# A decoder block on one core: tokens in the order of their expert groups, two tiles finished among the last pairs, rows moved by index

## The chip, the cores and the metric

One core of a Trainium2 chip runs the whole kernel in one launch. The metric is the device time of that launch in microseconds (us), the median of several runs. The engines are TensorE (PE in the profile), VectorE (DVE), ScalarE (ACT), GpSimd (POOL) and SyncE (SP), which here only starts transfers.

## The reference, cut to what matters

512 tokens of width 1024. Two token mixers come first (a chunked retention and a sliding-window attention); the change leaves them alone. Then a mixture of experts in two levels, and last a gated embedding per layer:

```python
g_sel = argmax(softmax(hf @ w_rg + b_rg))             # one of 4 groups
top_p, top_i = top_k(softmax(e_logits[g_sel]), 2)     # 2 of the 8 experts of that group
for grp in range(4):                                  # 8 experts each, D=1024, F=256
    hid = silu(hf @ w_gate) * (hf @ w_up)
    y += (hid * combine) @ w_down
x = x + y
ple = rms_norm(p @ w_ple, g)                          # p: 512 x 256
x = x + sigmoid(rms_norm(x, g2) @ w_ple_gate) * ple   # the gate product, 1024 x 1024
```

## The kernel before

**Stages.** The mixers and their output projection run until about 378 us; the result x1 (four tiles of 128 tokens) stays in SBUF and a copy of it goes to DRAM (`X1`). Then 16 pairs of experts (p_ = 0 to 15; pair p_ holds experts p_ and p_ + 16), then a tail with the gate product of the four tiles.

**A pair.** A pair has 64 slots for each of its two experts. Its 128 rows of x1 are gathered from `X1` by index on POOL (`fetch`, L1062), two pairs ahead. TensorE transposes them (`turn`, L1073), VectorE applies the gain (`turned`, `grow`, L962). `gu` (L1182) computes gate and up in plain fp32, the two experts in the two halves of the array's columns; `hidden` applies SiLU on ScalarE (L1195) and the product on VectorE (L1196); `ht` (L1203) transposes, VectorE copies (L1205); `down` (L1226) computes the output. For pairs 0 to 11 (`SC = 12`) ScalarE and VectorE copy the output (L1241, L1239) and POOL scatters its rows by index to `Y` in DRAM (L1246). For pairs 12 to 15 the output is split into a high and a low part in fp32r, and `combine` (L1256) brings its rows to the four token tiles by products with one-hot matrices, which `added` adds to x2 (L1269). In this kernel x2 is x1, tile by tile.

**Y.** In pair 12 `collect` clears eight tiles on VectorE (L1498) and gathers the rows of `Y` into them (L1503), two per token tile. POOL adds the two (`presum`, L1510), VectorE adds the sum to x2 (`total`, L1515).

**Embedding.** p arrives transposed (`pT`); `ple_split` splits it, and `embed(t)` computes p @ w_ple and its norm for one tile in each of the pairs 10 to 13 (twelve products of 512 columns in the split form, L1304 to L1306).

**Tail.** For each tile `tail_a` transposes x2 (L1430) and splits it (L1434, L1436), `tail_r` computes the norm, `tail_b` the gate product (L1456) in two halves of 512 columns as three fp32r products (high by high, low by high, high by low; 24 instructions for a half), `tail_c` applies the sigmoid (L1464) and writes the rows from SP (L1467). The gate weights (`wpg`, four loads of 1 MB) are split by `wpsplit` into two tiles of their own: ScalarE copies the high part (L1408), POOL (for the fourth VectorE) subtracts (L1410).

**What sets the order.** Each engine works in the order in which the program is written; waits are by semaphore. The weights come by SP in the order of `want`, each into a free place of SBUF as soon as the program frees one (`pump`, L322 and L324); `KEEP` sets places aside from a pair on, and `AT` and `at=` name places. A place that was another tile's makes the new writer wait for that tile's last user. `overflow` (L1321), after pair 0's gate product, is a branch for experts with more than 64 tokens, which is not taken here; SP reads a count for it, and its tiles have places of their own.

## Time and profile before

| | us |
|---|---|
| median of 3 runs | 692.26 (691.82 to 693.97) |
| the profiled execution | 694.86 |
| its span, first to last instruction | 693.1 |
| TensorE busy (share of the span) | 650.2 (94%) |
| VectorE, ScalarE, POOL busy | 319.5, 201.4, 91.9 |
| gate product of pair 0 starts | 378.78 |
| down of pair 15 starts | 628.90 |
| mean granted TensorE clock | 0.986 |

The timelines give for each piece of work its start, its length (matmuls overlap, so a group's length is up to 0.4 longer than the time to its successor), and how long the engine was idle before it and for whom. The waits add this up.

### The profile page before, as it was taken

To read this page: it belongs to the slowest core of one execution; us is meant where nothing else is said; L and a number is where in the kernel's file an instruction comes from. 1 tells how busy PE (TensorE), PEld (TensorE's weight loads), DVE (VectorE), ACT (ScalarE), POOL (GpSimd) and SP (SyncE) were. 2 spreads that over 40 slices of the span, in tenths; PEclk is the share of its full clock that TensorE was granted. 3 is DMA by queue.
4 is the path that set the end of the run, shared out by engine and by line. 5 is a ranking of instruction groups with operands and counts; after the bars stand their busy time and mean duration, and the time that the engine had idled before them with its cause. 6 is when DMAs were issued, how large, how long until landed. Compare 5 with 4: busy or idle time off the path is not lost. (4 is left out here: it accounts for less than half of the span.)

```text
span 693.1 us, 8410 instructions
## 1 busy us (share of the span) xinstructions
PE 650.2 (94%) x3210; PEld 441.8 (64%) x3210; DVE 319.5 (46%) x697; ACT 201.4 (29%) x393; POOL 91.9 (13%) x75
## 2 busy tenths in 40 slices
PE   7999999999999999999999699899879997998997
PEld 6768888778888888888887243333324443433886
DVE  5395556652456425635148121321202236566762
ACT  6664352363133334330142000000002110106431
POOL 1005000000001000000000121111105115417200
PEclk9999999999999999999999899999999999999999
DMA  8726310531204731049878489999999999992011
GB/s 282 283 85 238 143 61 1 182 122 62 114 22 169 304 122 61 0 183 354 347 293 341 152 305 415 420 418 421 418 421 421 414 374 413 417 415 90 31 47 45
DMA packets 32476, 162.98 MB, mean 235 GB/s; under 512 B 5577, under 2 KB 8265, under 8 KB 16304
## 3 DMA queue, kind: packets, MB, share of 16 engines
q1 hardware_dynamic: 26672, 149.90, 54.8%
q0 software_dynamic: 5040, 10.39, 4.0%
q10 hardware_dynamic: 720, 2.11, 0.8%
q8 instruction: 26, 0.43, 0.2%
q14 instruction: 18, 0.15, 0.1%
HBM read 155.67 MB, written 14.68 MB: 246 GB/s over the span
## 5 line engine op out<-in xcount | busy, mean ns | idle before, releaser
L431 PE MATMUL bank<-slab,slab 128*128 128x512 f32 x320 | 126.4, 395 | 0.0
L433 PE MATMUL bank<-slab,slab 128*128 128x512 f32 x320 | 124.9, 391 | 0.5 <-DVE slab L348 0.5
L1182 PE MATMUL bank<-slab,slab 128*64 128x512 f32 x512 | 119.9, 602 | 5.7 <-DMA slab<-wgu 4.2
L432 PE MATMUL bank<-slab,slab 128*128 128x512 f32 x320 | 125.0, 391 | 0.0
L1182 PEld LDWEIGHTS bank<-slab,slab 128*64 128x64 f32 x512 | 39.0, 138 | 80.1 <-issue 69.2
L348 DVE TENSOR_TENSOR slab<-slab,slab 128x1024 fp32r<-128x1024 f32 (+2 forms) x50 | 53.9, 1092 | 57.5 <-ACT slab L347 42.6
L431 PEld LDWEIGHTS bank<-slab,slab 128*128 128x128 f32 x320 | 60.1, 188 | 14.1 <-issue 1.8
L433 PEld LDWEIGHTS bank<-slab,slab 128*128 128x128 f32 x320 | 60.1, 188 | 13.6 <-DVE slab L348 1.0
L432 PEld LDWEIGHTS bank<-slab,slab 128*128 128x128 f32 x320 | 60.2, 188 | 11.6
L1226 PE MATMUL bank<-slab,slab 128*64 128x512 f32 x256 | 60.9, 618 | 5.1 <-DVE slab L1205 5.1
L347 ACT ACTIVATE slab<-slab 128x1024 fp32r<-128x1024 f32 (+2 forms) x50 | 46.4, 952 | 56.7 <-PE bank L432 26.1
L1196 DVE SCALAR_TENSOR_TENSOR slab<-slab,st,bank 128x256 f32<-128x256 f32 x16 | 7.7, 480 | 104.4 <-ACT slab L1195 104.4
L1195 ACT ACTIVATE slab<-bank,st 128x256 f32<-128x256 f32 x16 | 7.6, 474 | 146.2 <-PE bank L1182 138.5
L1456 PE MATMUL bank<-slab,slab 128*128 128x512 f32 (+1 forms) x216 | 45.9, 369 | 1.4 <-DVE slab L1436 1.4
L1456 PEld LDWEIGHTS bank<-slab,slab 128*128 128x128 f32 x216 | 37.0, 189 | 9.0 <-DVE slab L1436 2.3
L1226 PEld LDWEIGHTS bank<-slab,slab 128*64 128x64 f32 x256 | 18.3, 141 | 37.0 <-issue 36.3
L1062 POOL DMA_INDIRECT slab<-X,st x15 | 15.4, 1030 | 108.9 <-PE bank L1073 81.1
L880 PE MATMUL bank<-slab,slab 128*128 128x512 f32 x64 | 26.1, 408 | 0.0
L355 POOL TENSOR_TENSOR st<-st,ct 128x4 f32<-128x4 f32 x4 | 4.4, 1104 | 159.6 <-DVE st L354 159.6
L882 PE MATMUL bank<-slab,slab 128*128 128x512 f32 x64 | 25.0, 391 | 0.0
L881 PE MATMUL bank<-slab,slab 128*128 128x512 f32 x64 | 24.9, 390 | 0.0
L1239 DVE COPY slab<-bank 128x512 f32<-128x512 f32 x12 | 8.3, 692 | 34.6 <-PE bank L1226 34.6
(248 smaller groups left out, 924.5 us busy)
## 6 DMA issues: line engine op xcount, KB each, us to landing
slab<-wgu SPq DMA_DIRECT2D x64, 1024.0 KB, 13.9
slab<-wd SPq DMA_DIRECT2D x31, 1024.0 KB, 12.7
slab<-win SPq DMA_DIRECT2D x17, 1024.0 KB, 4.9
slab<-x SPq DMA_DIRECT2D x8, 512.0 KB, 6.1
Y<-slab SPq DMA_DIRECT2D x8, 512.0 KB, 4.9
slab<-wout SPq DMA_DIRECT2D x4, 1024.0 KB, 5.6
slab<-wpg SPq DMA_DIRECT2D x4, 1024.0 KB, 14.6
slab<-wso SPq DMA_DIRECT2D x2, 1024.0 KB, 6.1
```

Source lines behind the costliest of these rows:

```text
L347: A.activation(H.r(*shape), rawap, AF.Copy)
L348: (eng or V).tensor_tensor(L.r(*shape), rawap, H.f(*shape), op=OP.subtract)
L431: T.matmul(ps, wh[:, k, :], hh[k], start=(k == 0), stop=False)
L432: T.matmul(ps, wh[:, k, :], hl[k], start=False, stop=False)
L433: T.matmul(ps, wl[:, k, :], hh[k], start=False, stop=(k == nk - 1))
L880: T.matmul(ps, a, wh[:, kk, :], start=(k == 0), stop=False)
L881: T.matmul(ps, a, wl[:, kk, :], start=False, stop=False)
L882: T.matmul(ps, b, wh[:, kk, :], start=False, stop=(k == 7))
L1062: G.indirect_dma_start(out=XR[p_].f(1024), out_offset=None, in_=X1, in_offset=bass.IndirectOffsetOnAxis(ap=toki[:, p_:p_ + 1], axis=0), bo ...
L1182: T.matmul(b[j * 64:(j + 1) * 64, :], xg[:, k, j * 64:(j + 1) * 64], load(("gu", p_ + 16 * j, k // 4)).f(4, 512)[:, k % 4, :], start=(k == ...
L1226: T.matmul(bs[nh][j * 64:(j + 1) * 64, :], t.f(2, P)[:, f, j * 64:(j + 1) * 64], load(("wd", p_ + 16 * j)).f(2, 1024)[:, f, nh * 512:(nh + ...
L1456: T.matmul(b, (H, L, H)[i][:, k, :], w, start=(k, i) == terms[0], stop=(k, i) == terms[-1])
```

## The change

- **Pairs.** Pair p_ holds experts 2 p_ and 2 p_ + 1, so pairs 0 to 3 are group 0, and so on; the router's columns are no longer reordered. Tokens get a new order, by group: `order_a`, `order_b` and `order_c` (after pairs 2 and 3, and in pair 4) compute each token's place, the row index of each new tile (`permi`), the index of its `Y` rows (`yi`) and the place of every slot for the one-hot matrices.
- **Rows by index.** x1's tiles in SBUF are freed before pair 0. p is gathered by index (`ple_rows`) and transposed on TensorE (`ple_split`); embeddings move to pairs 7 to 9. x2 is gathered per new tile (`rows_x`), `Y` rows per tile (`rows_y`, two gathers): tile 0 in pair 9, tiles 1 and 2 in pair 12, tile 3 after pair 13; `total` adds both on POOL (tile 3: VectorE). The output rows are scattered by POOL.
- **Gate product of tile 0** after down in pairs 11 and 12 in plain fp32 from the raw weights (`tail_x`, `tail_b`, `tail_c`); tile 1's first half in pair 15.
- **Combine** only for tiles 2 and 3.
- **Weights.** `wpg` comes after pair 8 into places 42 to 57; `wpsplit` writes the low part over the raw weights and runs after pair 14 (0 and 1) and inside pair 15's gate product (2 and 3). `KEEP` begins earlier. `overflow`'s tiles have other places.

```diff
...
     SC = 12
-    KEEP = {9: (46, 74)}
-    AT = {("gu", 0, 1): 0, ("gu", 16, 1): 4, ("gu", 1, 0): 14, ("gu", 17, 1): 18}
-    LATE = (("gu", 16, 1),)
-    PL, PU = 8, (10, 11, 12, 13)
+    KEEP = {4: (58, 74), 6: (42, 82)}
+    AT = {("gu", 0, 1): 0, ("gu", 1, 1): 4, ("gu", 2, 0): 14, ("gu", 3, 1): 18}
+    LATE = (("gu", 1, 1),) + tuple(("wpg", i) for i in range(4)) + (("gple",), ("wple",))
+    PL, PU, PG = 5, {7: (0,), 8: (1, 2), 9: (3,)}, 8
...
     for p_ in range(16):
         for j in range(2):
-            for e in (p_, p_ + 16):
+            for e in (2 * p_, 2 * p_ + 1):
                 want(("gu", e, j), I["wgu"][e, j], 8, AT.get(("gu", e, j)))
-        for i in range(WE if p_ == 15 else 0):
-            want(("wpg", i), I["wpg"][i], 8)
-        for e in (p_, p_ + 16):
+        for e in (2 * p_, 2 * p_ + 1):
             want(("wd", e), I["wd"][e], 8)
         if p_ == PL:
-            want(("pT",), I["pT"], 4)
-            want(("gple",), 1024, 4)
-            want(("wple",), I["wple"], 8)
-    for i in range(WE, 4):
-        want(("wpg", i), I["wpg"][i], 8)
+            want(("gple",), 1024, 4, 60)
+            want(("wple",), I["wple"], 8, 62)
+        if p_ == PG:
+            for i in range(4):
+                want(("wpg", i), I["wpg"][i], 8, 42 + 4 * i)
...
+        for i in range(2):
+            V.tensor_reduce(few[:, i:i + 1], cb[:, 4 * NE:4 * NE + 16 + 8 * i], AX.X, OP.add)
+            V.tensor_scalar(few[:, i:i + 1], few[:, i:i + 1], 2 * P * (i + 1) - 0.5, float(SLOTS), op0=OP.is_lt, op1=OP.mult)
+        V.tensor_tensor(few[:, 2:3], few[:, 0:1], few[:, 1:2], op=OP.max)
+        V.tensor_scalar(cnt[:, 8:16], cnt[:, 8:16], few[:, 2:3], None, op0=OP.add)
...
+    for a in x1:
+        a.free()
+    pump(0)
...
         t = HT.pop(p_)
         last = p_ >= SC
         if last:
-            a = (50, 54)[p_ % 2]
+            a = (60, 64)[p_ % 2]
             H, L = ar.get(4, r=True, at=a), ar.get(4, r=True, at=a + 2)
             OT[p_] = ar.get(2, r=True, at=6 + p_ % 2)
-            V.tensor_scalar(OT[p_].r(512), io, tokf[:, p_:p_ + 1], None, op0=OP.is_equal)
+            V.tensor_scalar(OT[p_].r(256), io[:, 256:512], tokf[:, p_:p_ + 1], None, op0=OP.is_equal)
...
             for p_, i in terms:
-                T.matmul(CB[t][nh], OT[p_].r(512)[:, t * P:(t + 1) * P],
+                T.matmul(CB[t][nh], OT[p_].r(2, P)[:, t - 2, :],
...
+    def ple_rows():
+
+        pr = loaded[("p",)] = ar.get(4, at=16)
+        for t in range(4):
...
+        pr = loaded[("p",)]
+        H, L = ar.get(4, r=True, at=70), ar.get(4, r=True, at=72)
+        for k in range(2):
+            b = gb()
+            for t in range(4):
+                T.transpose(b[:, t * P:(t + 1) * P], pr.f(4, 2, P)[:, t, k, :], ident)
+            A.activation(H.r(2, 512)[:, k], b, AF.Copy)
+            V.tensor_sub(L.r(2, 512)[:, k], b, H.f(2, 512)[:, k])
+        pr.free()
+        PW.append((H, L))
+        raw = load(("wple",))
+        H = ar.get(8, r=True, at=66)
+        A.activation(H.r(2048), raw.f(2048), AF.Copy)
+        f = raw.f(2048)
+        L = ar.rounded(raw)
+        G.tensor_tensor(L.r(2048), f, H.f(2048), op=OP.subtract)
+        PW.append((H, L))
...
         gm, tb_, xg, h, xr, wb = (ar.get(kb, r=r, at=at) for kb, r, at in (
-            (2, True, 1), (4, False, 2), (4, False, 4), (2, False, 12), (4, False, 6), (4, False, 8)))
+            (2, True, 1), (4, False, 12), (4, False, 4), (2, False, 3), (4, False, 6), (4, False, 8)))
...
+    def wpsplit(i):
+
+        raw = load(("wpg", i))
+        f = raw.f(2, 1024)
+        H, L = Wp[i // 2, i % 2] = ar.get(8, r=True), ar.rounded(raw)
+        for k in range(2):
+            A.activation(H.r(2, 1024)[:, k], f[:, k], AF.Copy)
+            (G if i in WG else V).tensor_tensor(L.r(2, 1024)[:, k], f[:, k], H.f(2, 1024)[:, k], op=OP.subtract)
...
+    def tail_x(t, at):
+
         xs = x2[t].f(1024)
-        junk = ar.get(2, at=2 + t % 2)
+        HL[t] = [ar.get(4, at=at)]
+        for hb in range(2):
...
+    def tail_b(t, nh, lo=0, n=512, at=None):
+
         if nh == lo == 0:
-            OO[t] = ar.get(4, at=(0, 8)[t % 2])
+            OO[t] = ar.get(4, at=at)
         b = tmain()[:, 0:n]
-        terms = [(k, i) for k in range(8) for i in range(3)]
-        if t == nh == 0:
-            terms.sort(key=lambda x: (x[1] == 2, x[0] // 4, x[1]))
-        for k, i in terms:
-            w = Wp[nh, k // 4][i // 2].r(4, 512)[:, k % 4, lo:lo + n]
-            T.matmul(b, (H, L, H)[i][:, k, :], w, start=(k, i) == terms[0], stop=(k, i) == terms[-1])
+        if len(HL[t]) == 1:
+            for k in range(8):
+                T.matmul(b, HL[t][0].f(8, P)[:, k, :], load(("wpg", 2 * nh + k // 4)).f(4, 512)[:, k % 4, lo:lo + n],
+                         start=(k == 0), stop=(k == 7))
+        else:
...
-        Q.dma_start(out[t * P:(t + 1) * P, ns], s)
...
+        elif end:
+            G.indirect_dma_start(out=out, out_offset=bass.IndirectOffsetOnAxis(ap=permi[:, t:t + 1], axis=0),
+                                 in_=OO[t].f(1024), in_offset=None, bounds_check=S - 1, oob_is_err=False)
+        if end:
+            for a in (OO[t], *HL[t], x2[t], ple[t]):
+                a.free()
...
+    def order_a():
+
+        o_ = oh4.rearrange("p (g t) -> p g t", t=4)
+        for t in range(4):
+            V.tensor_scalar(o_[:, :, t], C("io32", 0, 4), GI[t][:, 0:1], None, op0=OP.is_equal)
+        b = gb()
+        T.matmul(b[:, 0:16], C("up"), oh4, start=True, stop=True)
+        T.matmul(b[:, 16:32], C("ones"), oh4, start=True, stop=True)
+        a, c, w = rt.f(16, o=1168), rt.f(16, o=1184), rt.f(16, o=1200)
+        V.tensor_copy(a, b[:, 16:32])
...
+    def order_b():
+
+
+        for i in range(8):
+            V.tensor_scalar(io[:, i * SLOTS:(i + 1) * SLOTS], C("io64"), i * SLOTS - 1.0, None, op0=OP.add)
+        for t in range(4):
+            SO.append(ar.get(2, at=16 + t))
+            V.tensor_scalar(SO[t].f(S), io, pos[:, t:t + 1], None, op0=OP.is_equal)
...
+    def order_c():
+
+        b, c = gb(), gb()
+        for q in range(4):
+            for t in range(4):
+                T.matmul(b[:, 3 * q:3 * q + 3], SO[t].f(4, P)[:, q, :], src3[:, 3 * t:3 * t + 3],
+                         start=(t == 0), stop=(t == 3))
         for t in range(4):
-            for i in range(2):
-                y = ar.get(4, at=58 + 4 * t + 2 * i)
-                V.memset(y.f(1024), 0.0)
...
-    def total(t):
-
-        V.tensor_tensor(x2[t].f(1024), x2[t].f(1024), YS[2 * t][1].f(1024), op=OP.add)
-        YS[2 * t][1].free()
-
-    io = rt.f(S, o=640)
+            T.matmul(c, src3[:, 3 * t:3 * t + 1].to_broadcast([P, P]), SO[t].f(S), start=(t == 0), stop=(t == 3))
...
+    YS = {}
+
+    def rows_x(t, at):
+
+        x2[t] = ar.get(4, at=at)
+        G.indirect_dma_start(out=x2[t].f(1024), out_offset=None, in_=X1,
+                             in_offset=bass.IndirectOffsetOnAxis(ap=permi[:, t:t + 1], axis=0),
+                             bounds_check=S - 1, oob_is_err=False)
+
+    def rows_y(t, ats):
+
+        YS[t] = [ar.get(4, at=a) for a in ats]
+        for i in range(2):
+            if t > 1:
+                G.memset(YS[t][i].f(1024), 0.0)
+            G.indirect_dma_start(out=YS[t][i].f(1024), out_offset=None, in_=Y,
+                                 in_offset=bass.IndirectOffsetOnAxis(ap=yi[:, 2 * t + i:2 * t + i + 1], axis=0),
+                                 bounds_check=2 * S - 1, oob_is_err=False)
...
+    def total(t, eng):
+
+        for a in YS[t]:
+            eng.tensor_tensor(x2[t].f(1024), x2[t].f(1024), a.f(1024), op=OP.add)
+            a.free()
...
     for p_ in range(16):
         if p_ in KEEP:
             ar.kept = set(range(*KEEP[p_]))
-        if p_ == SC:
-            for i in range(8):
-                V.tensor_scalar(io[:, i * SLOTS:(i + 1) * SLOTS], C("io64"), i * SLOTS - 1.0, None, op0=OP.add)
...
         if p_ > SC:
-            combine([p_ - 1], 0), combine([p_ - 1], 1)
+            combine([p_ - 1], 2, False)
+        if p_ == 15:
+            wpsplit(2), wpsplit(3)
+        if p_ == 11:
+            tail_x(0, 76)
+            tail_r(0, 80)
...
+        if p_ > 13:
+            added(2)
+        if p_ == 14:
+            tail_a(1, 74, (76, 78))
+            tail_r(1, 16)
         if p_ == 15:
-            wpsplit(0), wpsplit(1)
-        if p_ > SC:
-            combine([p_ - 1], 2, False)
+            tail_b(1, 0, at=74)
         ht(p_)
-        if p_ > SC:
+        if p_ == 13:
             added(2)
         turned(p_ + 1, turn(p_ + 1))
-        for t in range(4):
-            if PU[t] == p_:
-                embed(t)
+        for t in PU.get(p_, ()):
+            embed(t)
+        if p_ == 4:
+            order_c()
+        if p_ == 9:
+            rows_y(0, (76, 78)), rows_x(0, 74)
         if p_ == SC:
-            collect()
+            rows_y(1, (70, 72)), rows_x(1, 68), rows_x(2, 80), rows_x(3, 4)
         down(p_)
+        if p_ == 2:
+            order_a()
+        if p_ == 3:
+            order_b()
+        if p_ == 5:
+            ple_rows()
+        if p_ == 6:
+            ple_split()
+        if p_ == 10:
+            total(0, G)
+        if p_ in (11, 12):
+            tail_b(0, p_ - 11, at=78)
+            tail_c(0, p_ - 11)
         if SC < p_ < 15:
             combine([p_ - 1], 3)
...
-    ar.kept = set(range(58, 66))
+        if p_ == 13:
+            total(1, G), total(2, G)
+            rows_y(3, (70, 72))
+        if p_ == 12:
+            rows_y(2, (76, 78))
+        if p_ == 14:
+            wpsplit(0), wpsplit(1)
+            total(3, V)
+        if p_ == 15:
+            tail_c(1, 0)
+    ar.kept.clear()
     pump(0)
...
+    taux, tmain = Ring([4, 5]), Ring([0, 6, 7])
+    tail_b(1, 1)
+    combine([15], 2)
+    tail_a(2, 0, (8, 10))
+    combine([14, 15], 3, False)
+    tail_c(1, 1)
+    tail_b(2, 0, at=16)
+    tail_r(2, 2)
+    added(3)
+    tail_a(3, 0, (12, 14))
+    tail_c(2, 0)
+    tail_b(2, 1)
+    tail_r(3, 3)
+    tail_c(2, 1)
+    tail_b(3, 0, at=18)
+    tail_c(3, 0)
+    for lo in range(0, 512, LN):
+        tail_b(3, 1, lo, LN)
+        tail_c(3, 1, lo, LN)
```

Three places where the rows of an engine change, with what each waits for.

POOL, around the embeddings of pairs 9 and 10 (L1062 and L1064 fetch rows for a pair, L1246 and L1251 scatter a pair's output, L1278 and L1283 are the power in a norm). Before, from pair 10:

```order
L1278 TENSOR_TENSOR st<-st,ct 128x1 [waits DVE_49]
L1246 DMA Y<-slab_3801,st 1024x1024 [waits DMASW7_49,DVE_49,Activation_49]
L1062 DMA slab_3854<-X_76,st 128x1024 [waits DMASW6_49,PE_49]
L1278 TENSOR_TENSOR st<-st,ct 128x1 [waits DVE_49]
L1246 DMA Y<-slab_3881,st 1024x1024 [waits DMASW1_49,DVE_49,Activation_49]
```

The same engine now, from pair 9 to the norm of pair 11 (L1605 gathers `Y`, L1595 gathers x1, L1612 is `total`):

```order
L1283 TENSOR_TENSOR st<-st,ct 128x1 [waits DVE_49]
L1605 DMA slab_3899<-Y,st 128x1024 [waits DMAHW1_49,DMASW3_49,DMASW1_49]
L1605 DMA slab_3900<-Y,st 128x1024 [waits DMAHW2_49]
L1595 DMA slab_3907<-X_76,st 128x1024
L1251 DMA Y<-slab_3911,st 1024x1024 [waits DMASW3_49,DMASW4_49,DVE_49,Activation_49]
L1064 DMA slab_3968<-X_76,st 128x1024 [waits DMASW0_49,PE_49]
L1251 DMA Y<-slab_3975,st 1024x1024 [waits DMASW6_49,DVE_49,Activation_49]
L1612 TENSOR_TENSOR slab_3907<-slab_3907,slab_3899 128x1024 [waits DMASW5_49]
L1612 TENSOR_TENSOR slab_3907<-slab_3907,slab_3900 128x1024 [waits Pool_49]
```

Between the scatters of two pairs there are now three gathers, and behind pair 10's scatter the two sums of tile 0.

POOL, pairs 12 and 13. Before, the last gathers of `Y` and the sums:

```order
L1503 DMA slab_3985<-Y,st 128x1024 [waits DMAHW5_49,DVE_49]
L1503 DMA slab_3987<-Y,st 128x1024 [waits DMASW4_49,DVE_49]
L1278 TENSOR_TENSOR st<-st,ct 128x1 [waits DVE_49]
L1510 TENSOR_TENSOR slab_3973<-slab_3973,slab_3975 128x1024 [waits DMASW6_49,DMASW5_49]
L1510 TENSOR_TENSOR slab_3977<-slab_3977,slab_3979 128x1024 [waits DMASW7_49,DMASW0_49]
```

Now, from the last of three gathers of x1 on (L1511 writes tile 0's output, L1604 clears a tile):

```order
L1595 DMA slab_4150<-X_76,st 128x1024
L1511 DMA out_dram<-slab_4072,st 512x1024 [waits DMASW1_49,DVE_49,Activation_49]
L1604 MEMSET slab_4184 128x1024 [waits PE_49]
L1605 DMA slab_4184<-Y,st 128x1024 [waits Pool_49]
L1604 MEMSET slab_4185 128x1024 [waits DMASW1_49]
L1605 DMA slab_4185<-Y,st 128x1024 [waits DMASW3_49,Pool_49]
L1612 TENSOR_TENSOR slab_4142<-slab_4142,slab_4134 128x1024 [waits DMASW6_49,DMASW4_49]
L1612 TENSOR_TENSOR slab_4142<-slab_4142,slab_4135 128x1024 [waits DMASW5_49,Pool_49]
L1612 TENSOR_TENSOR slab_4146<-slab_4146,slab_4184 128x1024 [waits DMASW7_49,DMASW2_49,DVE_49]
L1612 TENSOR_TENSOR slab_4146<-slab_4146,slab_4185 128x1024 [waits DMASW3_49,Pool_49]
```

The output's scatter and two memsets stand among the gathers, and the second memset waits for a transfer (DMASW1, the output's).

ScalarE, pairs 14 and 15. Before, SiLU of pair 15 (L1195), then the high parts of two tiles of gate weights:

```order
L1195 ACTIVATE slab_4266<-bank0_68,st 128x256 [waits PE_49,Activation_49]
L1408 ACTIVATE slab_4269<-slab_4167 128x1024 [waits DMAHW3_49,DMAHW5_49,DMAHW2_49,DMAHW6_49,DMAHW1_49,DMAHW0_49]
L1408 ACTIVATE slab_4269<-slab_4167 128x1024
L1408 ACTIVATE slab_4275<-slab_4169 128x1024 [waits DMAHW3_49,DMAHW7_49,DMAHW1_49,DMAHW0_49]
L1408 ACTIVATE slab_4275<-slab_4169 128x1024
```

Now all four tiles (L1435) and then SiLU of pair 15 (L1200):

```order
L1435 ACTIVATE slab_4379<-slab_3659 128x1024 [waits DMAHW5_49,DMAHW4_49,DMAHW6_49,DMAHW3_49,DMAHW1_49]
L1435 ACTIVATE slab_4379<-slab_3659 128x1024 [waits Pool_49]
L1435 ACTIVATE slab_4385<-slab_3661 128x1024 [waits DMAHW7_49,DMAHW2_49]
L1435 ACTIVATE slab_4385<-slab_3661 128x1024 [waits Pool_49]
L1435 ACTIVATE slab_4405<-slab_3663 128x1024 [waits DMAHW0_49]
L1435 ACTIVATE slab_4405<-slab_3663 128x1024 [waits Pool_49]
L1435 ACTIVATE slab_4411<-slab_3665 128x1024 [waits DMAHW1_49,PE_49]
L1435 ACTIVATE slab_4411<-slab_3665 128x1024 [waits DVE_49]
L1200 ACTIVATE slab_4425<-bank0_68,st 128x256 [waits PE_49]
```

The copies have moved ahead of the SiLU, and the second of each tile waits for the engine that subtracts.

## Rows read from the trace of the kernel before

**Rows 1.** By stretch: length, busy PE, PEld, DVE, ACT, POOL; clock, DMA share, GB/s.
```profile
392.00:396.00 4.00, 3.03 (x8) 1.51 (x10) 0.42 (x1) 0.00 (x0) 1.00 (x1) 0.50 0.20 50
405.00:500.00 95.00, 86.04 (x427) 32.85 (x424) 21.83 (x43) 7.98 (x15) 14.29 (x14) 1.00 1.00 408
...
637.00:694.00 57.00, 49.90 (x252) 41.65 (x251) 34.42 (x50) 20.07 (x37) 8.53 (x7) 0.98 0.10 38
```
**Rows 2.** Waits of TensorE from 378 us on: in total, times, longest.
```profile
PE bank L1203 <- DVE slab L1196: 14.6, 13, 1.2
PE bank L1226 <- DVE slab L1205: 5.1, 2, 4.6
PE bank L1182 <- DMA slab<-wgu: 4.2, 3, 2.3
PE bank L1256 <- DVE slab L1219: 3.9, 1, 3.9
```
**Rows 3.** Timeline of TensorE, down of pairs 0 and 1: start, length, idle before.
```profile
392.97 6.04 PE L1226 MATMUL bank<-slab,slab 128*64 128x512 f32 x16 [4.56 <-DVE slab L1205]
...
410.05 3.65 PE L1226 MATMUL bank<-slab,slab 128*64 128x512 f32 x16
```
**Rows 4.** The same timeline, the rest of pairs 1 and 2.
```profile
409.06 1.06 PE L1073 MATMUL bank<-ct,slab 128*128 128x128 f32 x8
...
413.54 7.04 PE L1182 MATMUL bank<-slab,slab 128*64 128x512 f32 x32
```
**Rows 5.** The same timeline: plain fp32 (L526), a half gate product (L1456).
```profile
44.55 1.89 PE L526 MATMUL bank<-slab,ct 128*10 128x512 f32 x4
...
46.96 2.74 PE L526 MATMUL bank<-slab,ct 128*10 128x512 f32 x6
...
651.61 5.61 PE L1456 MATMUL bank<-slab,slab 128*128 128x512 f32 x24
```
**Rows 6.** Timeline of POOL, pairs 12 to 14: norm, first and last gather, last sum.
```profile
572.49 0.56 POOL L1278 TENSOR_TENSOR st<-st,ct 128x1 f32<-128x1 f32 x1 [3.44 <-DVE st L1277]
574.24 1.05 POOL L1503 DMA_INDIRECT slab<-Y,st  x1 [1.19 <-DVE slab L1498]
...
583.73 0.99 POOL L1503 DMA_INDIRECT slab<-Y,st  x1 [0.30 <-DVE slab L1269]
...
607.20 2.36 POOL L1510 TENSOR_TENSOR slab<-slab,slab 128x1024 f32<-128x1024 f32 x1 [2.19 <-DMA slab<-Y,st]
```
**Rows 7.** DMA issues from 378 us on: KB each, median us to landing.
```profile
out_dram<-slab SPq DMA_DIRECT2D x7, 256.0 KB, 2.0
...
Y<-slab,st POOLq DMA_INDIRECT x12, 8.3
slab<-Y,st POOLq DMA_INDIRECT x8, 15.8
```
**Rows 8.** Line L1503, the gathers of `Y`: landing.
```profile
DMA to landing us min/median/max: 9.4/15.8/23.3
```
**Rows 9.** Timeline of TensorE: down(12), the combines of pairs 12 and 13.
```profile
570.44 3.65 PE L1226 MATMUL bank<-slab,slab 128*64 128x512 f32 x16
...
581.42 3.77 PE L1256 MATMUL bank<-slab,slab 128*128 128x512 f32 x8 [3.90 <-DVE slab L1219]
...
603.51 2.24 PE L1256 MATMUL bank<-slab,slab 128*128 128x512 f32 x8
```
**Rows 10.** Timelines of ScalarE, POOL and VectorE in the tail.
```profile
627.28 3.89 ACT L1408 ACTIVATE slab<-slab 128x1024 fp32r<-128x1024 f32 x4
...
648.08 1.28 ACT L1464 ACT_TABLE_LOAD   x1
...
628.46 9.59 POOL L1410 TENSOR_TENSOR slab<-slab,slab 128x1024 fp32r<-128x1024 f32 x4 [18.90 <-DMA slab<-wpg]
...
636.70 4.70 DVE L1436 TENSOR_TENSOR slab<-slab,slab 128x512 fp32r<-128x512 f32 x2
...
660.81 1.30 DVE L1436 TENSOR_TENSOR slab<-slab,slab 128x512 fp32r<-128x512 f32 x2
```

196 lines of the change are left out of this document (87 added, 109 removed).

## Prediction

> **What bounds the kernel now.** I read the table of stages first, then the waits of TensorE, then the timelines of single pairs. The stages [rows 1] show two regimes. From 405 to 500 us TensorE is busy 86 of 95 us and the DMA share is 1.00 at 408 GB/s: computing and weight stream are level. From 637 to 694 us the DMA share is 0.10 and TensorE is busy 49.9 of 57 us: only computing counts. The waits of TensorE [rows 2] are small beside the 314 us of this part: 14.6 us in thirteen waits of 1.1 us (SiLU and product of each pair), and single ones that the change touches: 4.6 of the 5.1 us in pair 0, 4.2 us for `wgu`, 3.9 us for VectorE's eight memsets. So the kernel is bounded by TensorE with next to nothing in front of it, and a change can win by less TensorE work or by these few waits, and lose by any new wait. A pair takes 12.9 us on TensorE: gate and up 6.9 (7.04 with the overlap at its end), the wait 1.1, ten transposes 1.3, down 3.5 [rows 2 to 4].
>
> **The change part by part**, against the profiled execution (694.9 us; its span of 693.1 and 1.8 around it; 2.6 above the median of 692.3). I add differences and put them on the median.
>
> *Pair 0.* VectorE's copy L1205 waits until SP is past the overflow branch, because its tile lies where the branch's tile lay. `overflow` now takes place 12, so the wait goes to the operand of pair 1. TensorE's wait of 4.6 goes, and down ran for 6.04 behind it where it needs 3.65 [rows 3], since the granted clock had fallen while TensorE stood (0.50, the 1.2 GHz level, from 392 to 396 [rows 1]): −6.5; at least −3, if pair 1 keeps half.
>
> *Order of tokens.* `order_a` makes TensorE wait for a few small VectorE operations, like the SiLU wait: +1.2 [rows 2], with its two products +1.6. `order_c` has 16 products of three columns, each two instructions; the nearest row is the transposes at 0.12 each [rows 4], so 32 x 0.12 = 3.9; and four products of 512 columns in plain fp32, two instructions of 0.44 each [rows 5], 3.5. All stand between down and the next gate product, with nothing beside them: +7.4. `ple_split` adds eight transposes, +1.0. Sum +10. The p and X1 gathers add 2 MB to the stream, 5 us of DMA at 408 GB/s, but the 4.2 us for `wgu` is then waited for elsewhere or covered by the longer TensorE path; the places set aside leave nine 8 KB buffers in circulation from pair 6 on, where before it was ten, from pair 9 on (counted from `KEEP` and the placed tiles). I put −1, between −4 and +5.
>
> *Gate product of tile 0 among pairs 11 and 12.* The split form is 24 instructions in 5.45 us for one half (its 5.61 less the overlap at the end [rows 5]); the plain form is 8 x 2 x 0.44 = 7.0. Two halves: +3.2. `tail_c` there uses Sigmoid between SiLUs: each change of table is 1.28 [rows 10]. Most of it is covered by gate products; the one in front of pair 13's SiLU is not: +1.3.
>
> *Combine and memsets.* Tiles 0 and 1 leave `combine`: eight products take 2.2 us [rows 9], four pairs: −8.7. VectorE's memsets go to POOL: the wait of 3.9 goes, and the combine behind it, 3.77 where 2.24 is normal [rows 9]: −5.4.
>
> *New wait in pair 11.* Here I follow POOL's queue [rows 6, 7] and the first excerpt. In pair 9 it gets two Y gathers and one X1 gather; the Y scatter of pair 9 waits for them, the scatter of pair 10 for that one's landing, and behind it, on the same queue, stand the two sums of `total(0)`, which the transposes in the middle of pair 11's gate product need. Landing of a Y gather 15.8, of a scatter 8.3 [rows 7], issue 1.3 (seven from 574.24 to 583.73 [rows 6]), two sums 2 x 2.36 = 4.7: 30 us. The gathers stand on POOL behind the power of pair 9's embedding; the same step came at 572.49 in pair 12 of before, 2.1 after its down began [rows 6, 9]. From their issue to the transposes TensorE so has 0.9 of down(9), pair 10 whole (12.9) and half a gate product (3.5): 17.3. It would stand for 12.7; as some of that falls on waits for weights that the path has anyway (3 to 4 of such there, [rows 2]), I take 9. The floor is 2.5: even were every landing free, the scatter's issue and the two sums come after down(10), and take 1.3 + 4.7 against 3.5 of half a product. The upper end is 14 (a Y gather landed at up to 23.3 [rows 8]). A stand of this length cost 2.4 of slow clock in pair 0; I put 2: +11, bounds +2.5 and +16.
>
> *New waits in pairs 13 and 14.* In pair 12 POOL issues five gathers, then the scatter of tile 0's output, a memset, a gather, a memset that waits for the output's landing, and a last gather (second excerpt). The eight gathers of before, issued one after another, took from 574.24 to 607.20: 4.1 us each [rows 6]. Seven such transfers are 29 us, the last gather after them, with memset, issue and landing (at least 8), then `total(2)`: 2 x 2.4. That is 42 to 44 us after the first issue. VectorE's `added(2)` of pair 14 waits for that sum, and behind it on VectorE stand the copies that `tail_a(1)` needs and TensorE after them. The first issue comes some 1.5 after the transposes for pair 13. TensorE's work from there: 2 of down, plain gate product 7.0, pair 13 with two combines 15, pair 14's gate product with two combines 9: 33. That leaves 10, of it some 2 already in pair 13, where `added(2)` needs the gathered x1 of tile 2; with 2 of slow clock +12, bounds 0 and +18.
>
> *New wait in pair 15.* `wpsplit` now writes the low part over the raw weights. So ScalarE's second half waits for POOL's first (third excerpt), and a tile costs POOL, ScalarE, POOL in turn: 2.4 + 1.0 + 2.4 [rows 10], where before ScalarE ran ahead, four in 3.89. From down(14) that is 1.0 for the first copy, 5.8 for each of two tiles, 2.4 + 1.0 until ScalarE is done with the third; then the fourth, whose subtractions are VectorE's: 1.0 + 1.3 + 1.0 (two halves took VectorE 1.30 with POOL idle, and 4.70 beside POOL [rows 10]); then SiLU and product, 1.1: 20.4, with the hand-overs 21.5. TensorE's work to there: two combines 2.2, gate product 7.0, `tail_b(1, 0)` 5.45: 14.6. So `ht(15)` waits 7, six more than the usual 1.1, and down(15) then runs slow, up to 2.5 and the wait for its copy: +10, bounds +4 and +14.
>
> *Tail.* `combine([15], 0)` and its waits, some 2 us, go with `combine` above; the output rows go by POOL, each behind the last one's landing. Landing from SP is 2.0 [rows 7], a scatter's 8.3 with a full queue; the queue is empty by then, so +1.3, up to +6.
>
> Sum: −6.5 + 10 − 1 + 3.2 + 1.3 − 8.7 − 5.4 + 11 + 12 + 10 + 1.3 = +27.2. I take off 1 for waits of before in the tail that go: +26, which on the median gives **718 us**.
>
> **The rivals.**
> *The waits are hidden, and it is faster.* The change's plan is that POOL's sums and the splits end before TensorE arrives. For it: POOL is busy only 14.3 of 95 and 8.5 of 57 us [rows 1], and the lower bounds above. Price: without the terms of pairs 11, 13, 14 and 15 (33 us) the sum is −7: 685; with the DMA term at its best 682. It decides if the gathers of pair 9 land within some 10 us and a full tile's queue time is near 2 us instead of 4.1. Against it: the landings [rows 7] were taken in just such a queue, and the chain of pair 15 needs no DMA at all.
> *The gathers are quick, the chain of pair 15 remains.* With the queue of weights idle while TensorE stands, a gather may be nearer the 2.0 of an output than 8.3 or 15.8. Then pair 11 costs its floor of 2.5, pairs 13 and 14 some 2.5: 718 − 18 = 700. The Trainium skill (DMA: Bandwidth & Descriptors, Anatomy of one DMA) gives 2.0 us and the bytes at 436 GB/s for a DMA from GpSimd, which would be some 3.2 us for a tile of 0.5 MB, an estimate from that page; the trace differs with 8.3 to 15.8, so this has a small chance.
> *Worse:* the stands add up, each also starving the weight stream's release of buffers, toward the upper bounds: 735.
> *It doesn't do what it says:* the new count sends pairs 8 to 15 into the overflow branch if the first groups hold too few tokens. That would cost far over 50 us; worked out from the reference's inputs, the groups hold 133, 117, 134 and 128 tokens, which is enough, so I give it nothing.
>
> **How the numbers follow.** Forecast 718 (707 to 730): 0.60. Quick gathers, 700: 0.15. Faster, 685: 0.19. Worse: 0.06. From 684 to 731 the range leaves out half of the faster case and most of the worse one. This kernel's measurement tells 0.3% (2 us) from no change. Faster by more: 0.19; within: 0.05, the edge between the faster case and the quick gathers; slower by more: 0.76.
>
> **What would show it.** Right: TensorE's waits list a wait of some 9 us for POOL's sum before the transposes of tile 0 in pair 11, one of 6 to 9 us in pair 14 behind `added(2)`, one of 8 us before `ht(15)` with ScalarE waiting for POOL at every second copy, and slow clock behind each; pair 0 without its 4.6. Down(15) then ends some 46 us later than at 632.5, and what follows it is some 20 us shorter (three half gate products of 5.45, two combines, the waits of the splits). Wrong: pairs 11 to 15 without such waits, or a Y gather that lands in under 5 us.

## The result and the profile after

The changed kernel takes 719.0 us (716.3 to 724.5) where the kernel before takes 692.0 on the same chip: 1.039 times as long, 95% interval 1.033 to 1.046. A second measurement gave 720.1 (718.1 to 722.3), 1.038 (1.035 to 1.042). The profiled execution has a span of 718.7 us, 25.6 more than before.

TensorE's waits from 378 us on, in total, times, longest (before: [rows 2]):

```profile
PE bank L1208 <- DVE slab L1201: 25.6, 15, 8.5
PE bank L1467 <- POOL slab L1612: 7.8, 1, 7.8
PE bank L1231 <- DVE slab L1210: 3.6, 2, 2.7
PE bank L1187 <- DMA slab<-wgu: 1.7, 2, 1.5
```

The first line is the wait for SiLU and product, in pair 15 now 8.5; the second is pair 11's wait for the sums on POOL. The waits of 4.6 (pair 0) and 3.9 (memsets) are gone. The gain and the loss are read from the starts of the gate products: pair 1 starts at 392.87 (before 400.39), pair 5 at 457.46 (452.24), pair 9 at 518.45 (503.79, but three more embeddings are done by then), pair 11 at 549.03 (540.79), pair 12 at 583.32 (557.67), pair 13 at 603.41 (573.92; the memsets hit before just behind this), pair 15 at 645.18 (617.37), down(15) at 669.93 (628.90). From the start of down(15) to the end it is 48.8 us (before 64.2).

TensorE's timeline in the places that the prediction names, start, length, idle before and for whom (down of pair 0; order_c; pair 11; pairs 13, 14, 15; before: [rows 3, 4]):

```profile
387.74 3.75 PE L1231 MATMUL bank<-slab,slab 128*64 128x512 f32 x16 [0.56 <-issue]
...
443.54 4.96 PE L1576 MATMUL bank<-slab,slab 128*128 128x3 f32 x32
448.35 5.69 PE L1579 MATMUL bank<-slab,slab 128*128 128x512 f32 x8
453.97 3.65 PE L1231 MATMUL bank<-slab,slab 128*64 128x512 f32 x16
...
563.03 1.97 PE L1467 MATMUL bank<-ct,slab 128*128 128x128 f32 x8 [7.81 <-POOL slab L1612]
564.92 5.39 PE L1187 MATMUL bank<-slab,slab 128*64 128x512 f32 x16
...
614.23 0.44 PE L1208 MATMUL bank<-ct,slab 128*128 128x128 f32 x2 [2.46 <-DVE slab L1201]
...
616.43 5.24 PE L1231 MATMUL bank<-slab,slab 128*64 128x512 f32 x16
...
631.02 0.66 PE L1450 MATMUL bank<-ct,slab 128*128 128x128 f32 x4
632.87 0.66 PE L1450 MATMUL bank<-ct,slab 128*128 128x128 f32 x4 [1.19 <-DVE slab L1274]
...
637.46 6.67 PE L1231 MATMUL bank<-slab,slab 128*64 128x512 f32 x16 [2.74 <-DVE slab L1210]
...
668.40 0.69 PE L1208 MATMUL bank<-ct,slab 128*128 128x128 f32 x2 [8.45 <-DVE slab L1201]
669.93 5.79 PE L1231 MATMUL bank<-slab,slab 128*64 128x512 f32 x16 [0.84 <-DVE slab L1210]
```

Two things are to be seen. Long waits stand in pairs 11 and 15, where they were foretold; pair 14's, forecast at 6 to 9 us behind `added(2)`, are 1.19 and 2.74. And behind the waits of pairs 11, 13, 14 and 15 sixteen products that normally take 3.65 us take 5.2 to 6.7. By stretch (length, busy PE, PEld, DVE, ACT, POOL; granted clock, DMA share, GB/s) the clock is at 0.50, the 1.2 GHz level, in such a place (pair 15), and also from 446 to 452 us, where TensorE did not wait at all:

```profile
443.00:446.00 3.00, 3.00 (x28) 3.00 (x27) 1.58 (x3) 0.00 (x0) 1.02 (x1) 0.93 1.01 421
446.00:452.00 6.00, 6.00 (x17) 3.93 (x18) 0.43 (x5) 0.00 (x0) 0.00 (x0) 0.50 1.01 416
...
670.00:674.00 4.00, 4.00 (x10) 1.16 (x12) 0.14 (x1) 0.34 (x1) 0.00 (x0) 0.50 0.00 0
```

POOL's timeline, from the gathers of tile 0 to its sums, and from the first gather of pair 12 to the last sum of tile 2 (before: [rows 6]):

```profile
533.49 1.04 POOL L1605 DMA_INDIRECT slab<-Y,st  x1 [0.22 <-issue]
...
548.26 1.00 POOL L1251 DMA_INDIRECT Y<-slab,st  x1 [11.13 <-ACT slab L1246]
...
557.16 1.02 POOL L1251 DMA_INDIRECT Y<-slab,st  x1 [6.58 <-DMA Y<-slab,st]
558.21 4.76 POOL L1612 TENSOR_TENSOR slab<-slab,slab 128x1024 f32<-128x1024 f32 x2
...
594.45 1.01 POOL L1605 DMA_INDIRECT slab<-Y,st  x1 [0.31 <-issue]
...
606.53 1.02 POOL L1511 DMA_INDIRECT out_dram<-slab,st  x1 [5.85 <-issue]
...
616.13 0.95 POOL L1604 MEMSET slab<- 128x1024 f32 x1 [6.31 <-DMA out_dram<-slab,st]
617.35 1.01 POOL L1605 DMA_INDIRECT slab<-Y,st  x1 [0.27 <-POOL slab L1604]
...
626.83 2.36 POOL L1612 TENSOR_TENSOR slab<-slab,slab 128x1024 f32<-128x1024 f32 x1 [1.30 <-DMA slab<-Y,st]
```

The scatter of pair 9 is issued at 548.26, 14.8 us behind the first gather. The page puts its idle time down to a ScalarE copy, but that one (done at 547.8) belongs to pair 10; the copies of pair 9's output were done by 535.1, and the first excerpt of the section on the change lists two transfers that this scatter waits for as well. The next scatter waits 6.6 for its landing, and the sums end at 563.0, when TensorE goes on: 29.5 us from the first gather to the last sum, where the prediction had 30.

### The profile page after: what moved, and what is told of

Read it like the earlier page. It is cut to its first block, busy times and chain, and to the rows that moved or that the text cites. A ratio compares the mean times of both kernels' runs of the same rounds, so it can differ in the third digit from the quotient of the medians.

```text
span 718.7 us, 8419 instructions
## 1 busy us (share of the span) xinstructions
PE 658.8 (92%) x3214; PEld 442.4 (62%) x3214; DVE 303.5 (42%) x707; ACT 205.8 (29%) x396; POOL 112.0 (16%) x94
## 5 line engine op out<-in xcount | busy, mean ns | idle before, releaser
L428 PE MATMUL bank<-slab,slab 128*128 128x512 f32 x320 | 126.4, 395 | 0.0
L429 PE MATMUL bank<-slab,slab 128*128 128x512 f32 x320 | 124.9, 390 | 0.0
L430 PE MATMUL bank<-slab,slab 128*128 128x512 f32 x320 | 124.9, 391 | 0.0
L1187 PE MATMUL bank<-slab,slab 128*64 128x512 f32 x512 | 117.3, 602 | 3.0 <-DMA slab<-wgu 1.7
L1231 PE MATMUL bank<-slab,slab 128*64 128x512 f32 x256 | 66.4, 656 | 4.4 <-DVE slab L1210 3.6
L428 PEld LDWEIGHTS bank<-slab,slab 128*128 128x128 f32 x320 | 60.1, 188 | 13.9 <-issue 1.8
L430 PEld LDWEIGHTS bank<-slab,slab 128*128 128x128 f32 x320 | 60.1, 188 | 12.8 <-DVE slab L345 0.2
L429 PEld LDWEIGHTS bank<-slab,slab 128*128 128x128 f32 x320 | 60.2, 188 | 11.7
L1200 ACT ACTIVATE slab<-bank,st 128x256 f32<-128x256 f32 x16 | 7.6, 472 | 106.8 <-PE bank L1187 91.2
L1494 PE MATMUL bank<-slab,slab 128*128 128x512 f32 (+1 forms) x168 | 34.3, 362 | 0.4 <-POOL slab L1436 0.4
L1494 PEld LDWEIGHTS bank<-slab,slab 128*128 128x128 f32 x168 | 28.1, 189 | 7.0 <-issue 1.6
L1064 POOL DMA_INDIRECT slab<-X,st x15 | 15.5, 1034 | 97.9 <-PE bank L1075 69.4
L1208 PE MATMUL bank<-ct,slab 128*128 128x128 f32 x32 | 7.2, 308 | 25.6 <-DVE slab L1201 25.6
L1208 PEld LDWEIGHTS bank<-ct,slab 128*128 128x128 f32 x32 | 3.3, 144 | 38.4 <-DVE slab L1201 38.4
L877 PE MATMUL bank<-slab,slab 128*128 128x512 f32 x64 | 26.1, 408 | 0.0
L879 PE MATMUL bank<-slab,slab 128*128 128x512 f32 x64 | 25.0, 391 | 0.0
```

The costliest lines, as they stand in the source:

```text
L428: T.matmul(ps, wh[:, k, :], hh[k], start=(k == 0), stop=False)
L429: T.matmul(ps, wh[:, k, :], hl[k], start=False, stop=False)
L430: T.matmul(ps, wl[:, k, :], hh[k], start=False, stop=(k == nk - 1))
L877: T.matmul(ps, a, wh[:, kk, :], start=(k == 0), stop=False)
L879: T.matmul(ps, b, wh[:, kk, :], start=False, stop=(k == 7))
L1064: G.indirect_dma_start(out=XR[p_].f(1024), out_offset=None, in_=X1, in_offset=bass.IndirectOffsetOnAxis(ap=toki[:, p_:p_ + 1], axis=0), bo ...
```

## Experiments on the changed kernel

The kernel before, measured beside each of the runs below, took 692.0 to 693.3 us; differences between runs are good to about that.

**Split of the gate weights in two passes** (a_split). Both ScalarE copies of a tile first, then both subtractions.

```diff
         for k in range(2):
             A.activation(H.r(2, 1024)[:, k], f[:, k], AF.Copy)
+        for k in range(2):
             (G if i in WG else V).tensor_tensor(L.r(2, 1024)[:, k], f[:, k], H.f(2, 1024)[:, k], op=OP.subtract)
```

> The changed kernel with wpsplit in another order: both ScalarE copies of a tile of gate weights first, then both subtractions. Theory (ScalarE and POOL take turns because the low part is written over the raw weights): ScalarE's eight copies follow one another in some 8 us, SiLU of pair 15 no longer stands behind them, the wait of 8.45 us before the transposes of h in pair 15 falls to the usual 1.1 to 2.5 and the slow down behind it (5.79 us) to 3.6: 8 to 10 us less, 709 to 711 us. Rival (POOL's and VectorE's own time, or the sums of tile 3 on VectorE, set that wait): ScalarE is free early, but the wait stays above 6 us and the time within 3 us of 719.

Measured: 709.9 us (708.8 to 710.5), 1.024 of the kernel before (1.022 to 1.026): 9.1 less than the changed kernel. ScalarE's copies in pair 15 on the timeline of the changed kernel, on that of the split in two passes with the SiLU behind them, and TensorE's pair 15 of the latter:

```profile
648.20 2.01 ACT L1435 ACTIVATE slab<-slab 128x1024 fp32r<-128x1024 f32 x2 [2.48 <-POOL slab L1436]
...
665.64 1.06 ACT L1435 ACTIVATE slab<-slab 128x1024 fp32r<-128x1024 f32 x1 [2.59 <-DVE slab L1436]
```

```profile
644.52 7.68 ACT L1435 ACTIVATE slab<-slab 128x1024 fp32r<-128x1024 f32 x8
653.47 0.48 ACT L1200 ACTIVATE slab<-bank,st 128x256 f32<-128x256 f32 x1 [1.27 <-PE bank L1187]
```

```profile
660.48 0.44 PE L1208 MATMUL bank<-ct,slab 128*128 128x128 f32 x2 [0.26 <-DVE slab L1201]
662.01 3.65 PE L1231 MATMUL bank<-slab,slab 128*64 128x512 f32 x16 [1.09 <-DVE slab L1210]
```

The eight copies take 7.68 us instead of 22, the wait is 0.26 and down(15) runs at full clock. The theory holds; POOL's own time does not bound the pair.

**Tile 0's gathers one pair earlier** (a_pair8), and their sums after pair 9.

```diff
-        if p_ == 9:
+        if p_ == 8:
             rows_y(0, (76, 78)), rows_x(0, 74)
...
-        if p_ == 10:
+        if p_ == 9:
             total(0, G)
```

> The changed kernel with the gathers of tile 0 (two of Y, one of x1) in pair 8 and its sums after pair 9, one pair earlier each; their rows are complete after pair 7. Theory (pair 11 waits for the chain gathers, scatter of pair 9, scatter of pair 10, two sums): the wait of 7.81 us before tile 0's transposes and the half-speed products behind it go, 9 to 11 us less, 708 to 710 us. Rival (the weight stream, at a DMA share of 1.00 from 500 us on, has no room): the time reappears as waits for wgu in pairs 11 to 13, and less than 4 us are won.

Measured: 713.1 us (712.6 to 716.5), 1.030 (1.027 to 1.033): 5.9 less, between theory and rival. The wait of pair 11 is gone altogether, and part of it has come back further on:

```profile
555.43 1.09 PE L1467 MATMUL bank<-ct,slab 128*128 128x128 f32 x8
...
629.43 1.12 PE L1450 MATMUL bank<-ct,slab 128*128 128x128 f32 x4 [5.10 <-DVE slab L1274]
```

and on POOL's timeline the memset of the last gather's tile, behind the landing of the output:

```profile
616.33 0.95 POOL L1604 MEMSET slab<- 128x1024 f32 x1 [15.08 <-DMA out_dram<-slab,st]
```

The waits for `wgu` grew from 1.7 to 2.9, but most came back elsewhere than the rival said: the output of tile 0 took 18.4 us to land (597.97 to 616.33) instead of 9.6, the last gather behind it was late, pair 13 waited 1.9 for the gathered x1 of tile 2, and pair 14 waited 5.1 for `added(2)`, which on VectorE had itself waited 3.8 for POOL's sum. So here the chain of pair 12 that the prediction had described did bind: from its first issue (585.86) to the last sum (628.65) it took 42.8 us, and the prediction had 42 to 44.

The traces of the other runs say when. In the six executions in which pair 11 waits 7 us or more for its sums (the changed kernel twice, a_split, a_inter, a_y2b and a_late), the DMA share was 0.80 to 0.87 in the 14 us before the chain's first issue, and the chain took 34.4 to 35.6 us (32.3 in a_y2b, where its last gather does not wait for the output). In the three in which it doesn't the share was 1.01 and the chain took 42.8 (a_pair8), and 40.5 and 40.2 where that gather does not wait either (a_all, a_all2). That the slack in the weight stream, which follows TensorE's stand in pair 11, lets these gathers land sooner fits the numbers, but no run changes it alone.

**order_c interleaved** (a_inter), one wide product behind each four narrow ones.

```diff
         for q in range(4):
             for t in range(4):
                 T.matmul(b[:, 3 * q:3 * q + 3], ...)
-        for t in range(4):
-            T.matmul(c, src3[:, 3 * t:3 * t + 1].to_broadcast([P, P]), SO[t].f(S), ...)
+            T.matmul(c, src3[:, 3 * q:3 * q + 1].to_broadcast([P, P]), SO[q].f(S), ...)
```

> The changed kernel with order_c's four products of 512 columns put one behind each group of four three-column products, instead of all behind the last. Theory (the granted clock falls during the 32 three-column instructions, although TensorE is never idle there, and the four wide products then run at half speed): with wide products in between the clock stays at 1.00 and order_c takes 7.4 instead of 10.4 us, 2 to 3 us less. Rival (the wide products are slow of themselves, by their broadcast weights): order_c stays at 10 us or more and the wide instructions at 0.7 us each.

Measured: 713.1 us (711.6 to 714.6), 1.028 (1.026 to 1.031): 5.9 less. TensorE's timeline (the last of four such couples and the product behind it):

```profile
448.63 0.95 PE L1576 MATMUL bank<-slab,slab 128*128 128x3 f32 x8
449.44 1.10 PE L1578 MATMUL bank<-slab,slab 128*128 128x512 f32 x2
450.47 3.65 PE L1231 MATMUL bank<-slab,slab 128*64 128x512 f32 x16
```

The stretch that ran at 0.50 in the changed kernel (columns as above):

```profile
446.00:452.00 6.00, 6.00 (x31) 3.39 (x32) 1.12 (x6) 0.00 (x0) 0.00 (x0) 1.00 1.02 417
```

The clock stays at 1.00 here, order_c takes 7.1 us instead of 10.4 (10.4 to 12.1 in the six executions that have its products in the changed kernel's order), and a wide instruction 0.47 instead of 0.70 with the same broadcast weights: it was the clock, not the weights. That the interleaving keeps the clock up does not hold each time. Of three profiled executions with it two kept 1.00 (this one and a_all); in a_all2, below, the clock fell to 0.50 during the first wide product, and order_c took 12.8 us:

```profile
446.00:452.00 6.00, 6.00 (x17) 3.93 (x18) 0.00 (x0) 0.00 (x0) 0.00 (x0) 0.50 1.01 414
```

Of the 5.9 this stretch accounts for 3.3. The rest is in how long the clock stays low behind the later waits (down(14) 5.08 instead of 6.67, down(15) 5.00 instead of 5.79); that differs from execution to execution, and I don't put it down to the edit.

**Another place for the second Y tile of tile 2** (a_y2b), whose memset waited for the output's landing.

```diff
-            rows_y(2, (76, 78))
+            rows_y(2, (76, 16))
```

> The changed kernel with the second Y tile of tile 2 at place 16 (the embedding of tile 0, done by then) instead of 78 (tile 0's output). Its memset then no longer waits for the landing of that output. Theory (this wait of 6.3 us on POOL delays the last gather and both sums): the gather is issued 6 us earlier, total(2) ends some 4 to 6 us earlier, the waits of pair 14 (1.19 and 2.74 us) and the slow down (6.67 us) go, 3 to 6 us less. Rival (the shared gather queue sets the landing, whatever the issue): the gather lands within 2 us of where it did and the time stays within 2 us.

Measured: 717.8 us (715.1 to 719.7), 1.036 (1.032 to 1.039), 1.3 less than the first and 2.3 less than the second measurement of the changed kernel: not clear of its spread. The gather is issued 7.1 us earlier and the last sum ends at 625.9 instead of 629.2 (0.8 of both because this execution is that much ahead), but pair 14's two waits are still 1.19 and 2.74, to the hundredth:

```profile
636.66 5.00 PE L1231 MATMUL bank<-slab,slab 128*64 128x512 f32 x16 [2.74 <-DVE slab L1210]
```

Theory and rival were both beside the point: these waits are not made by POOL's sums. VectorE's timeline of the changed kernel in pair 14 shows what stands in front of the copy (L1210) that down needs: the two adds of `added(2)`, the two gains and two subtractions of `tail_a(1)`, and its norm, which waits for ScalarE:

```profile
632.13 1.28 DVE L1274 TENSOR_TENSOR slab<-slab,bank 128x512 f32<-128x512 f32 x2
633.33 1.28 DVE L1452 TENSOR_TENSOR slab<-bank,vec 128x512 f32<-128x512 f32 x2
634.76 1.29 DVE L1456 TENSOR_TENSOR slab<-slab,slab 128x512 fp32r<-128x512 f32 x2
636.67 0.21 DVE L1281 TENSOR_SCALAR st<-st 128x1 f32<-128x1 f32 x1 [0.62 <-ACT slab L1280]
...
636.99 0.41 DVE L1210 COPY slab<-bank 128x256 f32<-128x256 f32 x1
```

**tail_a(1) and its norm behind down(14)** (a_late), to see whether they are the cause.

```diff
-        if p_ > 13:
-            added(2)
-        if p_ == 14:
-            tail_a(1, 74, (76, 78))
-            tail_r(1, 16)
         if p_ == 15:
+            added(2)
             tail_b(1, 0, at=74)
         ht(p_)
-        if p_ == 13:
+        if p_ in (13, 14):
             added(2)
...
         if p_ == 14:
+            tail_a(1, 74, (76, 78))
+            tail_r(1, 16)
             wpsplit(0), wpsplit(1)
```

> The changed kernel with tail_a(1) and tail_r(1) of pair 14 moved behind down(14), and pair 14's second use of added(2) behind its transposes, as in pair 13. Theory now (the waits of pair 14, 1.19 and 2.74 us with a down of 5.0 to 6.7 us behind them, come from VectorE's own queue: two adds, two gains, two subtractions and a norm stand ahead of the copy that down needs; the sums on POOL had ended before): both waits go and down(14) takes 3.65 us, 4 to 7 us less than 719. Rival (the prediction's: the sums of tiles 1 and 2 come late): the wait reappears at tile 1's transposes or in added(2), less than 2 us.

Measured: 719.4 us (718.8 to 720.8), 1.039 (1.036 to 1.042): no difference. Pair 14 is as the theory said, and pair 15 gives it back:

```profile
632.73 3.65 PE L1231 MATMUL bank<-slab,slab 128*64 128x512 f32 x16
...
638.99 3.65 PE L1187 MATMUL bank<-slab,slab 128*64 128x512 f32 x16
...
656.73 1.21 PE L1494 MATMUL bank<-slab,slab 128*128 128x512 f32 x4 [1.70 <-POOL slab L1436]
666.38 0.69 PE L1208 MATMUL bank<-ct,slab 128*128 128x128 f32 x2 [8.44 <-DVE slab L1201]
```

Pair 15's gate product starts 6.2 us earlier (638.99), but the split's chain starts behind the moved copies and is as long as ever, so TensorE now also waits 3.8 us for the low parts and is at the transposes of h only 2.0 us earlier; down(15) then ran in 6.04.

**All four edits** (a_all; the first four diffs above together), and the four with the move of tail_a(1) (a_all2).

> The changed kernel with all four edits of the other experiments: split in two passes, tile 0's gathers a pair earlier, order_c interleaved, the second Y tile of tile 2 elsewhere. Theory (the change lost its gain to these waits): the sum of the four, 24 to 30 us less than 719, 689 to 695 us, about the kernel before. With the weight stream as the next limit (it ends some 35 us before down of pair 15 now) no part should come back. Rival: the gains overlap or new waits for wgu arise, over 703 us.

> The four edits of the run a_all and the move of tail_a(1) behind down(14). Theory: 4 to 6 us less than a_all's 700, 694 to 696 us; with x1 of tile 2 landing later than needed in pair 13 as before. Rival: the copies of tail_a(1) then stand in front of the split of the gate weights on ScalarE and move the wait to the last product of tail_b(1, 0) in pair 15, 698 us or more.

Measured: 700.3 us (698.9 to 704.4), 1.012 (1.009 to 1.016), and 701.6 (698.6 to 707.1), 1.011 (1.007 to 1.016). The four bring 18.7, between theory and rival, and less than the 22.2 that the single differences add up to (9.1 + 5.9 + 5.9 + 1.3) and than the 24 to 30 expected; pair 11 waits no more, pair 15 0.3, and the waits of pair 13 (2.46 and 1.68) and 14 (2.24 and 2.74) are left. The 2.24 is the chain of gathers again: its last sum ends at 623.3, and `added(2)`, for which the second half of tile 1's transposes waits, starts at 623.4. The move adds nothing, as its rival said: in pair 15 TensorE then waits for the low parts (0.45, 0.69 and 1.64 us, in the execution of 707.1, in which order_c ran slow too). So the change loses to the kernel before, by 1.2%, even with its longest waits mended.

## Experiments on the kernel before

Two parts of the change alone (b_ovf, b_mem), then both (b_both).

```diff
-            (2, True, 1), (4, False, 2), (4, False, 4), (2, False, 12), (4, False, 6), (4, False, 8)))
+            (2, True, 1), (4, False, 12), (4, False, 4), (2, False, 3), (4, False, 6), (4, False, 8)))
```

```diff
-                V.memset(y.f(1024), 0.0)
                 YS.append((t, y))
         for t in range(4):
             for i in range(2):
+                G.memset(YS[2 * t + i][1].f(1024), 0.0)
```

> The kernel before with one part of the change: the overflow branch's tiles at the changed kernel's places (12 instead of 2, 3 instead of 12). Theory: the wait of 4.6 us in pair 0 and the slow down behind it go (in the changed kernel pair 1 starts 6.3 us earlier against pair 0), and since the weight stream is at its limit from 405 us on, part of it comes back as waits for wgu: 2 to 6 us less than 692, 686 to 690 us. Rival (all of it comes back from the stream): within 1 us of 692.

> The kernel before with the eight clears of the Y tiles on POOL, each in front of its gather, instead of on VectorE. Theory: the wait of 3.9 us before the combine of pair 12 and the slow combine behind it go, POOL's 8 x 0.95 us are covered by the gathers' landing: 4.5 to 5.5 us less, 687 us. Rival (the later gathers delay the sums and x2): a new wait of several us in pair 14 or the tail, within 2 us of 692.

> The kernel before with both: overflow's tiles at the other places and the clears on POOL. If the two are independent the gains add: 7 to 11 us less than 692, 681 to 685 us. If the weight stream takes them back, waits for wgu from pair 8 on grow and the gain is that of the clears alone.

Measured: 687.3 us (ratio 0.992, 0.990 to 0.995), 687.1 (0.992, 0.990 to 0.994), and both 681.6 (680.4 to 682.1; 0.983, 0.980 to 0.985). They add, 5.6 + 5.8 = 11.4 against 11.3, and the last beats both kernels. TensorE's waits with both:

```profile
PE bank L1203 <- DVE slab L1196: 14.6, 13, 1.2
PE bank L1182 <- DMA slab<-wgu: 4.5, 4, 2.2
```

The waits for `wgu` went from 4.2 to 4.5 and those for `wd` from none to 1.0: the stream, at a share of 1.00, took back 1.3 at most.

**Transposes for the next pair ahead of those of h** (b_turn), on that kernel. In pairs 13 to 15 they overwrite a bank of `combine` before it is added, so tile 2 lacks part of its sum there; the amount of work is the same.

```diff
+        bs = turn(p_ + 1)
         ht(p_)
         if p_ > SC:
             added(2)
-        turned(p_ + 1, turn(p_ + 1))
+        turned(p_ + 1, bs)
```

> The kernel of b_both (before, with overflow's tiles elsewhere and the clears on POOL), and in pairs 1 to 15 the eight transposes for the next pair put in front of the two of h, into the wait of 1.1 us for SiLU and product. If TensorE alone bounds the pairs, each pair is 0.9 us shorter: 10 to 12 us less than 681.6, 670 us. If the weight stream bounds them (its share is 1.00 from 400 to 600 us in b_both, with 4.5 us of waits for wgu left), the time comes back as waits for wgu and wd: 3 us or less, 679 us.

Measured: 682.2 us (681.4 to 685.0), no gain, as the second case had it. But the timeline of pair 2 shows that most of it is not the stream:

```profile
412.49 1.09 PE L1073 MATMUL bank<-ct,slab 128*128 128x128 f32 x8
413.71 0.44 PE L1203 MATMUL bank<-ct,slab 128*128 128x128 f32 x2
414.76 3.65 PE L1226 MATMUL bank<-slab,slab 128*64 128x512 f32 x16 [0.61 <-DVE slab L1205]
```

The wait of 1.1 is filled, but down now follows the transposes of h directly and waits for VectorE's copy of them, which the other eight transposes used to cover: the pair is 12.7 us long instead of 12.9. Of those 0.2 a pair, the waits for `wgu` take the rest (7.4 instead of 4.5).

**The changed kernel once more** (a_again).

> The changed kernel once more, for the spread of its own runs: 719 us, 716 to 724. If the differences of the single edits to it (5.9 us for order_c interleaved, of which its stretch shows 3.5) are real to a microsecond, the median repeats within 1 us; if its runs scatter by how long the clock stays low behind each wait, it moves by 1 to 3 us.

Measured: 720.1 us, given above, 1.1 from the first, at the edge between the two cases. In both measurements the runs with the lower mean clock are the longer ones (0.971 at 716.3 and 717.6 us, 0.964 at 724.5). In the profiled execution pair 1 also waited 1.5 for its gathered rows and its down took 5.35.

## Why the prediction was right

718 was forecast and 719 measured. By its steps, from the profiled executions:

- *Pair 0* (−6.5): pair 1 starts 15.3 us behind pair 0 instead of 21.6, −6.3. b_ovf shows it alone, −5.6.
- *Order of tokens* (+10): mis-sized. Pair 2 with `order_a` +2.1 (1.6 forecast), `ple_split`'s transposes +1.1 (1.0), but `order_c` 10.4 for 7.4. The instructions were priced rightly (7.1 in a_inter, at full clock); the price took full clock for granted.
- *Stream* (−1): the waits for `wgu` and `wd` are 2.0 in all, −2.2.
- *Plain fp32* (+3.2): a half takes 7.06 us, as said. *Change of table* (+1.3): pair 13's SiLU wait is 2.46, +1.4 on the usual.
- *Combine and memsets* (−8.7, −5.4): 32 products of `combine` remain of 64, at 1.1 for four; b_mem shows the memsets' part alone, −5.8.
- *Pair 11* (+11): 7.8 of wait, and 1.0 and 1.7 of slow clock behind it: +10.5, by the chain described (it took 29.5 us for the 30 forecast, TensorE's work to there 21.7 for 17.3). a_pair8 takes the wait away by an earlier start of that chain.
- *Pairs 13 and 14* (+12): this step failed in its cause. The chain of gathers took 34.7 us from the first issue to the last sum, not 42 to 44: the memset of the last tile waited for six transfers and not for seven, they landed in 21.7 us (3.6 each instead of 4.1), the last one landed in some 9.5, and one of the two last sums was done by then. It ended at 629.2, before TensorE came to the transposes at 631.0, 36.6 us after the first issue and not 33. What was there instead is VectorE's and ScalarE's own queue: two adds, two gains, two subtractions and a norm in front of the copy that down needs, 1.2 and 2.2 more than usual (a_y2b leaves them as they were, a_late removes them), with 1.6 (in pair 13, behind its wait of 2.46) and 3.0 of slow clock: +8. Taking away the 6.2 of it that stand in pair 14 (a_late) gains nothing clear of the spread, since pair 15's chain takes some 4 of them back. The terms were also added up as if each stood alone: with pair 11's wait gone, the chain takes its 42.8 us and binds (a_pair8).
- *Pair 15* (+10): 7.4 of wait above the usual 1.1, 0.3 for the copy, 2.1 of slow down: +9.8, and a_split takes back 9.1. From down(14) to the transposes of h it was 24.3 us by the split's chain (21.5 forecast) and 15.9 of TensorE's work (14.6).
- *Tail* (+1.3): mis-sized. From the last product to the end it takes 10.0 us instead of 4.8, +5.2: each of the last two outputs waits on POOL for the landing of the one before, 2.3 us at the last, and from the last issue to the end it is 5.9 (712.84 to 718.7) where from SP's it was 3.2 (689.9 to 693.1). The scatter itself is not the most of it: its bytes have moved by 714.8. What ends last is a DRAIN in POOL's own queue behind it, 5.3 us long, until 717.9; before, the same instruction took 3.5 and was over by 680.3.

The misses (+3 in order_c, −1 in the stream, −4 in pairs 13 and 14, +4 in the tail) come to +2 together; the forecast's closeness of 1 us is luck in that. Of its signs, the waits of pairs 11 and 15 came as described and that of pair 14 did not; down(15) ended 43 us later and not 46, and what follows it was 18 us shorter and not 20.

The rival of quick gathers did not come: the first gathers of tile 0 held the queue for 14.8 us. The faster rival priced the kernel without its new waits at 685; a_all, with the long ones gone, is at 700. Of the difference some 7, counted in the same way, are what is left in pairs 13 and 14, waits and slow clock, and 4 the tail above its price; the rest is not worked out.
